# A hybrid decoder layer: the mixer's planned order, its state update and its DMA places are changed

## The chip, the cores and the metric

The kernel runs on one core of a Trainium2 chip. The metric is the time of one execution on the device, in microseconds (us). Lower is better.

## The reference

One layer on x of 1024 tokens by 1024 columns, all in float32, in this order:

```python
x = layer_norm(ALPHA * x + 0.5 * swiglu(x, ffn1_w_gu, ffn1_w_down))       # FFN 1, inner width 2816
z = x @ w_in                                                              # 3872 columns
# retention, 8 heads of 64, chunks of 128 tokens
scores = einsum('bnihd,bnjhd->bnhij', q, k) * intra                       # decay mask
state  = chunk_decay * state + einsum('bnjhd,bnjhe,hj->nbhde', k, v, k_decay)
ret    = scores @ v + (q * q_decay) @ previous_state                      # group norm, gate
# RWKV-7, 8 heads of 64, token by token
sa     = einsum('bhvk,bhk->bhv', state, kk)
state  = state * w - sa (x) (kk * a) + v (x) k
y      = einsum('bhvk,bhk->bhv', state, r)                                # group norm, bonus, gate
x = layer_norm(ALPHA * x + concat(ret, rw) @ w_out)
x = layer_norm(ALPHA * x + 0.5 * swiglu(x, ffn2_w_gu, ffn2_w_down))       # FFN 2
x = x + sigmoid(x @ ple_w_gate + b) * (p @ ple_w_proj)
```

kk is the key, scaled by rw_k_k and normalised to length 1 in each head: for that the squares of 64 columns are summed.

## The kernel before

Large products run as three float32r matmuls of high and low parts (mm3, lines 64 to 66); each operand is split by a ScalarE cast (line 50) and a VectorE or GpSimd subtraction (line 51). The two FFNs stand ahead of and behind the mixer, and the change doesn't touch them. The mixer lies at about 712 to 1584 us of the profiled span.

**Units.** Two heads and half of the sequence (512 tokens) make a unit, named w0_0 to w3_1 for RWKV and r0_0 to r3_1 for retention. A unit of RWKV is computed in four chunks of 128 tokens. For it the kernel needs, in this order:

- rw_inputs: the shifted mix of z, the decay, the squares of k (sq, line 1013), a matmul over them (line 1017), the normalised kk.
- rw_operands: the matmul m1p (line 1055) whose masked result M1 (line 1057) is a strictly lower triangle for each chunk and head; transposes of v, b and k (line 1069).
- substitution: inverts the 32 diagonal blocks of 32x32 of I - M1. M1 goes to a scratch in DRAM (line 1080) and comes back block by block (ilt, line 1084); 31 steps of two VectorE instructions follow (lines 1093 and 1095); the result ix goes to a second scratch (scs, line 1098).
- doublings: brings the blocks back into Xd (line 1108), transposes them on VectorE (line 1110) and joins them into the inverse of 128x128 by five groups of small matmuls, i1 to i5 (lines 1118 to 1140).
- rw_chunks, for each chunk: scores (lines 1152 and 1155), rhs (lines 1185 and 1188, copied by ScalarE on line 1190), sa = inverse times rhs (line 1194, copied on line 1196), the new state (lines 1200 and 1201), the output Y (lines 1213 to 1218). The state is kept in three tiles wst. The new one is fe * (PSUM + old state): ScalarE scales the old state (sf, line 1209), VectorE scales the PSUM result and adds (line 1210). The PSUM tile ch of a chunk holds rhs, sa, the state and Y side by side in one bank.
- rw_tail: group norm, transposes (ytp), the gate; the result goes to DRAM (mixed, line 1238).

**Fillers.** The projection z (28 column blocks of 48 matmuls, z_fill) and, after it, the product with w_out (wopo, 384 matmuls, w_out_fill) are cut into small pieces. w_out_fill loads its operands (line 1254) from mixed and w_out, splits them into mw, and adds each tile to xacc, which w_out loads from x1 (8 DMAs of 512 KB, line 1334).

**What sets the order.** The mixer's parts are generators. A `yield n` says that the part wants to go on n us later, on a planned clock that counts TensorE's work alone. The loop in `mixer` takes the part with the lowest rank that is due: 0 is the recurrence (doublings, chunks, tail), 1 the inputs and operands of the next unit, 2 the retention, -1 the substitution. Work done adds SHARE times its planned length to a debt, and while there is debt, or nothing is due, a piece of filler is taken. URGENT gives the instructions of a rank a higher or a lower priority for the scheduler that orders VectorE, ScalarE, GpSimd and the DMA queue. TensorE's instructions stay in the planned order. SP issues nearly all DMAs, in order: one that waits for its buffer holds back those behind it.

Of the kernel before, what the change touches and what calls it, by code (L numbers as in the profile page):

```python
# [28 lines left out]
SHARE = 0.65  # L29
URGENT = {-1: -60, 0: 60}  # L30


class Layer:
# [761 lines left out]
    def lora(self, zd, h):  # L795

        nc = self.nc
        sl = slice(h * HALF, (h + 1) * HALF)
        sg = []
        for i, (mu, omu) in enumerate(((self.pc("mu", 12), self.pc("omu", 12)), (self.pc("mu", 13), self.pc("omu", 13)),  # L800
                                       (self.pc("mu2"), self.pc("omu2")))):
            z = self.load_z(f"zl{i}_{h}", zd[i], h)
            t = self.ring("t", f"lt{i}_{h}")
            d = self.ring("t", f"ld{i}_{h}")
            self.shift_mix(d, z, mu, omu, t)
            if i == 0:
                nc.scalar.activation(d[0:64], d[0:64], AF.Tanh)
                nc.sync.dma_start(self.lor[:, sl], d)
            else:
                nc.scalar.activation(t, d, AF.Tanh, scale=0.5)  # L810
                nc.vector.tensor_scalar(out=d, in0=t, scalar1=0.5, scalar2=0.5, op0=ALU.mult, op1=ALU.add)
                sg.append(d)
        yield 8
        up = [self.mb.tile([P, HALF], F32, tag=t, name=f"gup{t}{h}", bufs=1) for t in ("zq", "zk")]
        nc.sync.dma_start(up[0], self.A["rw_g_up"][0][0:P])
        nc.gpsimd.memset(up[1][0:96], 0.0)
        nc.sync.dma_start(up[1][96:128], self.A["rw_g_up"][0][P:])
        for u in range(4):
            us = slice(u * P, (u + 1) * P)
            ps = self.ptile("sc", f"gps{u}_{h}", 2)  # L820
            for i in range(2):
                nc.tensor.matmul(ps, up[i][:, us], sg[i], start=i == 0, stop=i == 1)
            g = self.ring("c", f"gs{u}_{h}")
            nc.scalar.copy(g, ps)
            nc.sync.dma_start(self.gates[u][:, sl], g)
            yield 1
# [29 lines left out]
    def retention(self, u, h, zd, out):  # L856
# [83 lines left out]
        yield 9  # L940
# [14 lines left out]
    def rw_inputs(self, W, n, u, h, zd):  # L955
# [21 lines left out]
        k, r, v = m  # L977

# [33 lines left out]
        sq = tmp("sq")  # L1012
        nc.scalar.activation(sq, k, AF.Square, scale=self.pc("rw_k_k", u))
# [60 lines left out]
    def substitution(self, w):  # L1074
# [10 lines left out]
        yield 6  # L1085
# [3 lines left out]
        for j in range(B - 1):  # L1089
# [6 lines left out]
            yield 0.95  # L1096
        w.scr2 = self.dpool.tile([4, 8, B, B], F32, tag="scr2", name=f"scs{nm}", bufs=2)
        nc.sync.dma_start(w.scr2.rearrange("b s i j -> (b s) i j"), x)
        w.inverse = True
        self.substituting = False  # L1100

    def doublings(self, w):
# [3 lines left out]
        for b in range(4):  # L1106
            bs = slice(B * b, B * b + B)
            nc.sync.dma_start(self.Xd[bs, :, bs], w.scr2[b].rearrange("s i j -> i s j"))
# [6 lines left out]
        yield 8  # L1115
# [48 lines left out]
    def rw_chunks(self, w, out):  # L1164
# [6 lines left out]
        yr = self.ring("c", f"yr{nm}")  # L1171
        yield 3
        for c in range(4):
# [4 lines left out]
            if h == 1 and c == 0:  # L1178
                for e in range(2):
                    rr = slice(64 * e, 64 * e + 64)  # L1180
                    nc.vector.tensor_scalar(out=st[rr, rr], in0=st[rr, rr], scalar1=w.fm[rr, 0:1], scalar2=None, op0=ALU.mult)
# [17 lines left out]
            if not (h == 1 and c == 3):  # L1199
                nc.tensor.matmul(ch[:, 2 * P:3 * P], kt[:, cs], vt[:, cs], start=True, stop=False)  # L1200
                nc.tensor.matmul(ch[:, 2 * P:3 * P], bt[:, cs], sa, start=False, stop=True)
                for e in range(2):
                    rr = slice(64 * e, 64 * e + 64)
                    ps = ch[rr, 2 * P + 64 * e:2 * P + 64 * e + 64]
                    if first:
                        nc.vector.tensor_scalar(out=nx[rr, rr], in0=ps, scalar1=fe[rr, c:c + 1], scalar2=None, op0=ALU.mult)
                    else:
                        sf = mb.tile([P, 64], F32, tag="sf", name=f"sf{nm}{c}{e}", bufs=2)
                        nc.scalar.activation(sf[rr], st[rr, rr], AF.Copy, scale=fe[rr, c:c + 1])
                        nc.vector.scalar_tensor_tensor(out=nx[rr, rr], in0=ps, scalar=fe[rr, c:c + 1], in1=sf[rr],  # L1210
                                                       op0=ALU.mult, op1=ALU.add)
# [9 lines left out]
            yield 2.4  # L1221
# [3 lines left out]
    def rw_tail(self, w, yr, out):  # L1225
# [3 lines left out]
        yield 9  # L1229
# [8 lines left out]
        nc.sync.dma_start(out[:, sl], t)  # L1238
# [10 lines left out]
    def w_out_operand(self, kind, i, half, src):  # L1249
# [3 lines left out]
        raw = self.w_out_raw(f"wo{self.uid()}")  # L1253
        self.nc.sync.dma_start(raw, src)
# [3 lines left out]
    def w_out_fill(self, blocks, mixed, finish):  # L1258
# [4 lines left out]
        def operands(b):  # L1263
# [3 lines left out]
            if (ks, h) not in m:  # L1267
                m[ks, h] = [self.w_out_operand(0, i, h, mixed[k][:, h * HALF:(h + 1) * HALF]) for i, k in enumerate(ks)]
# [6 lines left out]
        yield 6  # L1275
# [9 lines left out]
        finish()  # L1285
# [3 lines left out]
        yield 5  # L1289
# [16 lines left out]
    def mixer(self, x1T, zs, mixed, x1, normalise):  # L1306
# [4 lines left out]
        with self.pool("zp") as zp, self.pool("mc") as mc, self.pool("mb") as mb, self.pool("mp", space=PSUM) as mp:  # L1311
# [7 lines left out]
            self.zdone, self.mixed_done = set(), set()  # L1319
            self.tail_done, self.hold, self.substituting = True, False, False  # L1320
# [8 lines left out]
            def w_out():  # L1329
# [3 lines left out]
                for t in range(TT):  # L1333
                    nc.sync.dma_start(self.xacc[t], x1[t * P:(t + 1) * P, :])
                yield from self.w_out_fill([(ks, h, n) for ks in ((4, 0), (5, 1), (6, 2), (7, 3)) for h in range(2)
# [67 lines left out]
            for s in range(-1, 9):  # L1403
# [14 lines left out]
                while any(t[1] in main for t in threads):  # L1418
# [3 lines left out]
                    if fg and (fready <= clock and (not able or debt > 0)):  # L1422
# [298 lines left out]
```

## Time and profile before

| | us |
|---|---|
| median of 3 runs | 2368.34 |
| lowest, highest | 2363.91, 2370.89 |
| profiled execution | 2372.27 |
| its span (first to last instruction) | 2370.20 |
| mean granted TensorE clock, share of full speed | 0.964 |

The profile names instructions by line, engine, operation and tile. A float32 matmul is recorded as two instructions, a float32r matmul or a transpose as one. A matmul's own duration overlaps the next one's: what it takes from TensorE is read from one start to the next. "Idle before" is time in which an engine stood still, put down to the releaser that came last. [...]

### The profile page before, as it was taken

How to read it: one execution, taken by the hardware profiler on the slowest of the kernel's cores; microseconds unless marked ns; L12 is line 12 of the kernel's file. 1: busy time of each engine (PE TensorE's matmuls, PEld its weight loads, DVE VectorE, ACT ScalarE, POOL GpSimd, SP SyncE). 2: the span in 40 equal slices, each digit the busy share in tenths (PEclk: the TensorE clock that was granted, in tenths of full speed). 3: DMA queues.
4: the chain of work that ended last, by engine and by line, in shares of the span. 5: the costliest groups of instructions: out<-in, count | busy, mean ns of one | idle time of the engine just before them, and what ended most of it. 6: DMA issues, size and time to landing. Idle time of an engine off the chain costs nothing.

```text
span 2370.2 us, 31197 instructions
## 1 busy us (share of the span) xinstructions
PE 2206.1 (93%) x11009; PEld 1793.0 (76%) x11009; DVE 1654.7 (70%) x2825; ACT 867.7 (37%) x1514; POOL 491.7 (21%) x384
## 2 busy tenths in 40 slices
PE   7999999999998989898998869778999999999999
PEld 5888888788785767776776757656888888788777
DVE  7777777665782477667757669769777767866862
ACT  4332323244643424324324323244323232445550
POOL 3345454100111000000000000016554553000220
PEclk9999999999999999999898879889999999999999
DMA  4355555597245433343243352032455554975321
GB/s 143 121 169 189 168 173 165 182 323 231 68 162 168 143 104 109 100 119 117 76 122 119 93 161 89 26 131 83 153 191 161 190 164 134 351 256 155 111 76 41
DMA packets 288963, 345.97 MB, mean 146 GB/s; under 512 B 35715, under 2 KB 162150, under 8 KB 288806
## 3 DMA queue, kind: packets, MB, share of 16 engines
q1 hardware_dynamic: 284224, 331.34, 43.7%
q0 software_dynamic: 3328, 12.06, 1.3%
q8 instruction: 87, 1.43, 0.3%
q10 hardware_dynamic: 1254, 0.58, 0.1%
q14 instruction: 70, 0.57, 0.1%
HBM read 237.47 MB, written 106.43 MB: 145 GB/s over the span
## 4 chain that ended last, share of the span: by engine, by line
PE 45%; DVE 11%; DMA 4%; ACT 3%; issue 2%; SPq 0%; POOL 0%; DVEq 0%; POOLq 0%; ACTq 0%
PE f2m L64 4%; PE f2m L65 3%; PE f2m L66 3%; PE z L64 3%; PE z L65 3%; PE z L66 3%; DMA f2w<-in_ffn_w_gu 2%; PE f2qa L65 1%; PE f2qa L66 1%; PE f2qa L64 1%; PE pg L65 1%; PE pg L64 1%; PE pg L66 1%; PE wopo L64 1%; PE wopo L65 1%
## 5 line engine op out<-in xcount | busy, mean ns | idle before, releaser
L64 PE MATMUL z<-x1Th,win_0h 128*128 128x512 f32 x224 | 103.2, 461 | 0.0
L64 PE MATMUL z<-x1Th,win_1h 128*128 128x512 f32 x224 | 100.2, 447 | 0.0
L66 PE MATMUL z<-x1Th,win_0l 128*128 128x512 f32 x224 | 91.5, 409 | 0.9 <-DVE win_0l L51 0.9
L65 PE MATMUL z<-x1Tl,win_0h 128*128 128x512 f32 x224 | 91.3, 407 | 0.0
L65 PE MATMUL z<-x1Tl,win_1h 128*128 128x512 f32 x224 | 91.1, 407 | 0.0
L66 PE MATMUL z<-x1Th,win_1l 128*128 128x512 f32 x224 | 91.1, 407 | 0.0
L152 POOL TENSOR_TENSOR f2tb<-f2tb,f2tb 128x512 f32<-128x512 f32 x44 | 70.5, 1601 | 91.6 <-DMA f2tb<-in_ffn_w_down 86.6
L51 DVE TENSOR_TENSOR f1hl<-f1s,f1hh 128x512 fp32r<-128x512 f32 x63 | 45.6, 723 | 61.7 <-ACT f1hh L50 61.7
L1095 DVE TENSOR_TENSOR ixw<-ixw,itw 32x31 f32<-32x31 f32 (+15 forms) x248 | 81.5, 329 | 6.2
L1093 DVE TENSOR_TENSOR itw<-iltw,ixw 32x31 f32<-32x31 f32 (+15 forms) x248 | 81.0, 327 | 6.3 <-issue 0.7
L64 PE MATMUL wopo<-mw 128*128 128x512 f32 x128 | 55.9, 437 | 23.9 <-ACT mw L50 23.7
L51 DVE TENSOR_TENSOR f2hl<-f2s,f2hh 128x512 fp32r<-128x512 f32 x63 | 45.0, 715 | 45.8 <-ACT f2hh L50 45.8
L1087 POOL MEMSET ixw<- 32x1024 f32 x8 | 7.5, 943 | 325.5 <-DMA scsw<-ixw 325.5
L50 ACT CAST f1hh<-f1s 128x512 fp32r<-128x512 f32 x63 | 39.2, 622 | 91.8 <-PE f1qa L65 38.3
L50 ACT CAST f2hh<-f2s 128x512 fp32r<-128x512 f32 x63 | 39.2, 623 | 90.4 <-PE f2qa L65 35.9
L152 POOL TENSOR_TENSOR f1tb<-f1tb,f1tb 128x512 f32<-128x512 f32 x44 | 64.8, 1474 | 32.6 <-DMA f1tb<-in_ffn_w_down 24.6
L111 DVE TENSOR_TENSOR f2S<-f2w 128x512 f32<-128x512 f32 x22 | 20.8, 947 | 65.1 <-DMA f2w<-in_ffn_w_gu 65.1
L65 PE MATMUL f2qa<-f2vl,f2hh 128*128 128x512 f32 x164 | 64.0, 390 | 0.5 <-DVE f2vl L51 0.5
L66 PE MATMUL f2qa<-f2vh,f2hl 128*128 128x512 f32 x164 | 63.9, 390 | 0.0
L65 PE MATMUL f1qa<-f1vl,f1hh 128*128 128x512 f32 x164 | 63.9, 389 | 0.0
L66 PE MATMUL f1qa<-f1vh,f1hl 128*128 128x512 f32 x164 | 63.8, 389 | 0.0
L182 DVE TENSOR_TENSOR f1U<-f1m,f1U 128x512 f32<-128x512 f32 x50 | 33.5, 687 | 42.7 <-PE f1m L66 42.6
(792 smaller groups left out, 7215.8 us busy)
## 6 DMA issues: line engine op xcount, KB each, us to landing
f1w<-in_ffn_w_gu SPq DMA_DIRECT2D x44, 512.0 KB
f2w<-in_ffn_w_gu SPq DMA_DIRECT2D x44, 512.0 KB
f1s<-hd SPq DMA_DIRECT2D x63, 256.0 KB
f2s<-hd SPq DMA_DIRECT2D x63, 256.0 KB
zs<-zs SPq DMA_DIRECT2D x56, 256.0 KB
raw_win<-in_w_in SPq DMA_DIRECT2D x54, 256.0 KB
f1tb<-in_ffn_w_down SPq DMA_DIRECT2D x44, 256.0 KB
wt<-f1tb SPq DMA_DIRECT2D x44, 256.0 KB
```

The source lines that it names most:

```text
L50: self.last_split = self.nc.scalar.copy(hi, src).ins
L51: (eng or self.nc.vector).tensor_tensor(out=lo, in0=src, in1=hi, op=ALU.subtract)
L64: mm(ps, a[0], b[0], start=first, stop=False)
L65: mm(ps, a[0], b[1], start=False, stop=False)
L66: mm(ps, a[1], b[0], start=False, stop=last)
L111: sub = lambda o, a, b, op=ALU.subtract: V.tensor_tensor(out=o, in0=a, in1=b, op=op)
L152: nc.gpsimd.tensor_tensor(out=t, in0=a, in1=b, op=ALU.subtract)
L182: add = lambda out, a, b, eng=V: eng.tensor_tensor(out=out, in0=a, in1=b, op=ALU.add)
L1087: nc.gpsimd.memset(x, 0.0)
L1093: nc.vector.tensor_tensor(out=t, in0=lt[:, j, j + 1:].unsqueeze(2).broadcast_to([B, n, c]), in1=x[:, j:j + 1, 0:c].broadcast_to([B, n, c]) ...
L1095: nc.vector.tensor_tensor(out=x[:, j + 1:, 0:c], in0=x[:, j + 1:, 0:c], in1=t, op=ALU.add)
```

## The change

- The planner: SHARE falls from 0.65 to 0.4; the substitution loses its lowered priority (-60); a filler piece is no longer taken for debt while a part of rank 0 is due; and nine of the `yield` values differ or go.
- sq is made in rw_inputs right behind the shifted mix, ahead of the `yield 4`.
- The loads into Xd are issued at the end of substitution, right behind the write of the second scratch, with `yield 12` behind them. They were at the head of doublings, with `yield 8`.
- The old state is added in PSUM, by a matmul with the identity (line 1203 of the changed kernel), and ScalarE writes the new state from PSUM with the scale fe (line 1207): two instructions of 64x64. sf and the two VectorE instructions go.
- The scaling of the state by fm at the start of a half is issued before the `yield 3`.
- The x1 loads into xacc are issued on GpSimd's queue, behind the first four operand loads of w_out.
- The last unit's output stays in SBUF (self.kept) and is split from there. The layer norm of the first half (finish) is issued behind the last operands.

```diff
-SHARE = 0.65
-URGENT = {-1: -60, 0: 60}
+SHARE = 0.4
+URGENT = {0: 60}
...
-        yield 8
+        yield 8 if h else 18
...
         k, r, v = m
+        sq = tmp("sq")
+        nc.scalar.activation(sq, k, AF.Square, scale=self.pc("rw_k_k", u))
 
         yield 4
...
-        yield 6
+        yield 8
         x = mb.tile([B, B, B], F32, tag="ix", name=f"ix{nm}", bufs=1)
...
-            yield 0.95
+            yield 0.4
         w.scr2 = self.dpool.tile([4, 8, B, B], F32, tag="scr2", name=f"scs{nm}", bufs=2)
         nc.sync.dma_start(w.scr2.rearrange("b s i j -> (b s) i j"), x)
...
+            nc.sync.dma_start(self.Xd[bs, :, bs], w.scr2[b].rearrange("s i j -> i s j"))
+        yield 12
+        w.inverse = True
...
-        yield 8
         ps = self.ptile("sc", f"i1{nm}", 2)
...
+                if not first:
+                    nc.tensor.matmul(ch[:, 2 * P:3 * P], self.ident, st, start=False, stop=False)
                 nc.tensor.matmul(ch[:, 2 * P:3 * P], bt[:, cs], sa, start=False, stop=True)
                 for e in range(2):
                     rr = slice(64 * e, 64 * e + 64)
-                    ps = ch[rr, 2 * P + 64 * e:2 * P + 64 * e + 64]
-                    if first:
-                        nc.vector.tensor_scalar(out=nx[rr, rr], in0=ps, scalar1=fe[rr, c:c + 1], scalar2=None, op0=ALU.mult)
-                    else:
-                        sf = mb.tile([P, 64], F32, tag="sf", name=f"sf{nm}{c}{e}", bufs=2)
-                        nc.scalar.activation(sf[rr], st[rr, rr], AF.Copy, scale=fe[rr, c:c + 1])
-                        nc.vector.scalar_tensor_tensor(out=nx[rr, rr], in0=ps, scalar=fe[rr, c:c + 1], in1=sf[rr],
-                                                       op0=ALU.mult, op1=ALU.add)
+                    nc.scalar.activation(nx[rr, rr], ch[rr, 2 * P + 64 * e:2 * P + 64 * e + 64], AF.Copy, scale=fe[rr, c:c + 1])
...
-        nc.sync.dma_start(out[:, sl], t)
+        if (u, h) == (3, 1):
+            self.kept = t
+        else:
+            nc.sync.dma_start(out[:, sl], t)
...
-        yield 6
+        residual()
+        yield 9
...
-        finish()
         while not ready(last):
             yield 1
         operands(last)
-        yield 5
+        finish()
+        yield 4
...
+                        nc.gpsimd.dma_start(self.xacc[t], x1[t * P:(t + 1) * P, :])
...
-                    if fg and (fready <= clock and (not able or debt > 0)):
+                    if fg and fready <= clock and (not able or debt > 0 and all(t[0] for t in able)):
```

Three places show what the change moves. On TensorE, in the second chunk of unit w0_0, before (kt and vt are token-major operands, bt the b vectors, arw the decayed keys and queries, scz the masked scores):

```order
L1200 MATMUL chw0_01_7747<-wvtw0_0_6785,wktw0_0_6826 128x128
L1201 MATMUL chw0_01_7747<-saw0_01_7777,wbtw0_0_6804 128x128
L1213 MATMUL chw0_01_7747<-wst1_6159,arw0_0_6717 128x128
L1217 MATMUL chw0_01_7747<-wvtw0_0_6785,scz2_6151 128x64
L1218 MATMUL chw0_01_7747<-saw0_01_7777,scz2_6151 128x64
```

And now:

```order
L1201 MATMUL chw0_01_7654<-wvtw0_0_6812,wktw0_0_6852 128x128
L1203 MATMUL chw0_01_7654<-wst1_6159,ident_58 128x128
L1204 MATMUL chw0_01_7654<-saw0_01_7691,wbtw0_0_6836 128x128
L1209 MATMUL chw0_01_7654<-wst1_6159,arw0_0_6746 128x128
L1213 MATMUL chw0_01_7654<-wvtw0_0_6812,scz2_6151 128x64
L1214 MATMUL chw0_01_7654<-saw0_01_7691,scz2_6151 128x64
```

One matmul with the identity (line 1203) is new; there are 24 of them, one for each chunk that has an old state and makes a new one. Line 1209 waited for VectorE (as line 1213 of before) and now waits for ScalarE.

On ScalarE, in the third chunk of unit w0_1, before (sa is the copy that line 1201 needs, yr the output's):

```order
L1196 COPY saw0_12_8652<-chw0_12_8626 128x128
L792 ACTIVATE smkw2_0_9124<-wzkw2_0_9120,pder_1851 128x512
L1219 COPY yrw0_1_8330<-chw0_12_8626 128x128
L50 CAST win2304_1h_8707<-raw_win2304_1_8618 128x512
L690 COPY zs2816_1_8701<-z2816_1_8506 128x512
```

And now:

```order
L1197 COPY saw0_12_8506<-chw0_12_8469 128x128
L842 ACTIVATE gsqr0_1_8455<-gnyr0_1_8451 128x512
L50 CAST win1664_1h_8534<-raw_win1664_1_8396 128x512
L690 COPY zs1152_1_8531<-z1152_1_8170 128x512
L844 ACTIVATE gstr0_1_8450<-gstr0_1_8450,col2_7327 128x8
L938 ACT_TABLE_LOAD
L938 ACTIVATE rthr0_1_8463<-zgr0_1_8461 128x512
L1207 ACTIVATE wst1_6159<-chw0_12_8469,few0_1_6960 64x64 x2
L1215 COPY yrw0_1_8139<-chw0_12_8469 128x128
```

The state copies (line 1207) stand behind the retention's group norm and a table load.

On SP's queue, around the second scratch of unit w2_1, before (scs is the scratch, ix the inverted blocks):

```order
L966 DMA lor0w3_1_11410<-lor_6167 128x512
L882 DMA zvr2_1_11200<-zs_65 128x512
L1234 DMA gtw2_0_11266<-gates_6168 128x512
L664 DMA raw_win1920_0_11252<-in_w_in 128x4x128
L1036 DMA bv_6169<-rkw3_0_11100 128x512
L691 DMA zs_65<-zs896_0_11208 128x512
L787 DMA wzvw3_1_11427<-zs_65 128x513
L1098 DMA scsw2_1_11102<-ixw2_1_10518 32x1024
L691 DMA zs_65<-zs896_1_11223 128x512
L664 DMA raw_win1920_1_11474<-in_w_in 128x4x128
L1108 DMA Xd_6143<-scsw2_1_11102 32x8x32 x4
```

And now:

```order
L787 DMA wzrw3_1_11399<-zs_65 128x513
L968 DMA lorww3_1_11390<-in_rw_w_up 64x128
L969 DMA lorww3_1_11390<-in_rw_a_up 64x128
L1098 DMA scsw2_1_10771<-ixw2_1_10495 32x1024
L1228 DMA bvw2_0_11074<-bv_6169 128x512
L1101 DMA Xd_6143<-scsw2_1_10771 32x8x32 x2
L1230 DMA gtw2_0_11076<-gates_6168 128x512
L1101 DMA Xd_6143<-scsw2_1_10771 32x8x32 x2
L871 DMA zqr2_1_11185<-zs_65 128x512
```

The write of the scratch no longer stands behind the loads of the unit's tail (gtw) and the next unit's (lor0w, zvr), and the Xd loads follow it with two DMAs of others between.

## Rows read from the trace of the kernel before

**Rows 1.** The windows view of the mixer; columns: stretch, length, busy us, clock, DMA, GB/s.

```profile
712.00:1584.00 872.00, 754.55 (x4564) 602.55 (x4563) 578.63 (x1348) 297.72 (x589) 20.47 (x61) 0.92 0.37 113
```

**Rows 2.** The waits of TensorE in the mixer: us in total, times, longest.

```profile
PE wopo L64 <- ACT mw L50: 23.7, 2, 16.9
PE i1w L1118 <- DMA Xd<-scsw: 23.1, 8, 9.9
PE chw L1213 <- DVE wst L1210: 20.0, 24, 1.2
PE sspw L1017 <- ACT sqw L1013: 19.2, 8, 4.2
PE gps L822 <- DMA raw_win<-in_w_in: 7.7, 1, 7.7
PE ytpw L853 <- DVE gnyw L846: 4.8, 1, 4.8
```

**Rows 3.** The windows view of stretches right behind five of these waits.

```profile
733.70:742.00 8.30, 8.21 (x16) 4.14 (x17) 2.69 (x4) 3.35 (x7) 0.00 (x0) 0.66 0.49 170
1386.70:1397.00 10.30, 10.02 (x32) 7.69 (x33) 7.00 (x12) 1.46 (x3) 1.09 (x2) 0.61 0.33 88
1556.80:1571.00 14.20, 7.38 (x23) 5.72 (x24) 5.57 (x8) 1.24 (x2) 0.00 (x0) 0.58 0.71 204
1342.00:1352.00 10.00, 9.95 (x41) 8.72 (x42) 6.88 (x19) 2.77 (x5) 0.00 (x0) 0.58 0.20 62
993.00:1000.00 7.00, 6.78 (x30) 6.19 (x32) 5.07 (x15) 2.74 (x6) 0.00 (x0) 0.59 0.14 45
```

**Rows 4.** TensorE's timeline in one chunk: start, us, line, tiles, idle before.

```profile
1352.72 0.39 PE L66 MATMUL z<-x1Th,win_0l 128*128 128x512 f32 x1
1352.95 0.38 PE L1200 MATMUL chw<-wvtw,wktw 128*128 128x128 f32 x2
1353.17 0.39 PE L1201 MATMUL chw<-saw,wbtw 128*128 128x128 f32 x2
1354.32 0.49 PE L1213 MATMUL chw<-wst,arw 128*128 128x128 f32 x2 [0.76 <-DVE wst L1210]
```

**Rows 5.** The state's tile wst, two of its groups: ns min/median/max, first and last start.

```profile
L1209 ACT ACTIVATE sfw<-wst,few x48: 335/344/348, 907.2 to 1539.1; 64x64 f32<-64x64 f32 x48
L1210 DVE SCALAR_TENSOR_TENSOR wst<-chw,few,sfw x48: 261/284/292, 918.0 to 1545.5; 64x64 f32<-64x64 f32 x48
```

**Rows 6.** ScalarE's groups in the mixer, one table load of several groups: busy, mean ns.

```profile
L1019 ACT ACT_TABLE_LOAD x8 | 10.3, 1283 | 0.1
```

**Rows 7.** The page's groups of the substitution's two instructions: busy, mean ns.

```profile
L1095 DVE TENSOR_TENSOR ixw<-ixw,itw 32x31 f32<-32x31 f32 (+15 forms) x248 | 81.5, 329 | 6.2
L1093 DVE TENSOR_TENSOR itw<-iltw,ixw 32x31 f32<-32x31 f32 (+15 forms) x248 | 81.0, 327 | 6.3 <-issue 0.7
```

**Rows 8.** VectorE's timeline, unit w0_0: first and last step, the transpose of Xd.

```profile
833.30 0.17 DVE L1093 TENSOR_TENSOR itw<-iltw,ixw 32x31 f32<-32x31 f32 x1
...
873.07 0.18 DVE L1095 TENSOR_TENSOR ixw<-ixw,itw 32x31 f32<-32x31 f32 x1
878.94 1.25 DVE L1110 STREAM_TRANSPOSE XTw<-Xd 128x1024 f32<-128x1024 f32 x1 [5.68 <-DMA Xd<-scsw]
```

**Rows 9.** VectorE's timeline, unit w2_1: the last step of its substitution.

```profile
1275.39 0.18 DVE L1095 TENSOR_TENSOR ixw<-ixw,itw 32x31 f32<-32x31 f32 x1
```

**Rows 10.** SP's timeline, unit w2_1: the second scratch and the loads into Xd.

```profile
1291.65 0.58 SPq L1098 DMA_DIRECT2D scsw<-ixw  x1
...
1296.19 1.81 SPq L1108 DMA_DIRECT2D Xd<-scsw  x4
```

**Rows 11.** The chain that ended last, at the mixer's end: start, us, what.

```profile
1559.51 1.99 DMA mixed<-wow
...
1561.51 2.50 DMA wo<-mixed
```

**Rows 12.** The windows view around the start of w_out.

```profile
1366.00:1400.00 34.00, 16.40 (x68) 13.16 (x69) 15.72 (x28) 7.43 (x15) 1.09 (x2) 0.65 0.65 200
```

More of the change, by code (lines that the diff above doesn't have):

```diff
@@ L939, in retention @@
         nc.vector.scalar_tensor_tensor(out=th, in0=th, scalar=1.0, in1=zg, op0=ALU.add, op1=ALU.mult)
-        yield 9
+        yield 12
         yt = self.transposes(y, f"ytp{nm}")
@@ L1010, in rw_inputs @@
         nc.vector.tensor_scalar(out=ath, in0=ath, scalar1=0.5, scalar2=0.5, op0=ALU.mult, op1=ALU.add)
-        sq = tmp("sq")
-        nc.scalar.activation(sq, k, AF.Square, scale=self.pc("rw_k_k", u))
         yield 5
@@ L1095, in substitution @@
             nc.vector.tensor_tensor(out=x[:, j + 1:, 0:c], in0=x[:, j + 1:, 0:c], in1=t, op=ALU.add)
-            yield 0.95
+            yield 0.4
         w.scr2 = self.dpool.tile([4, 8, B, B], F32, tag="scr2", name=f"scs{nm}", bufs=2)
         nc.sync.dma_start(w.scr2.rearrange("b s i j -> (b s) i j"), x)
+        for b in range(4):
+            bs = slice(B * b, B * b + B)
+            nc.sync.dma_start(self.Xd[bs, :, bs], w.scr2[b].rearrange("s i j -> i s j"))
+        yield 12
         w.inverse = True
@@ L1105, in doublings @@
         B = 32
-        for b in range(4):
-            bs = slice(B * b, B * b + B)
-            nc.sync.dma_start(self.Xd[bs, :, bs], w.scr2[b].rearrange("s i j -> i s j"))
         XT = mb.tile([P, 8, P], F32, tag="XT", name=f"XT{nm}", bufs=1)
@@ L1171, in rw_chunks @@
         yr = self.ring("c", f"yr{nm}")
+        if h == 1:
+            st = self.wst[4 % 3]
+            for e in range(2):
+                rr = slice(64 * e, 64 * e + 64)
+                nc.vector.tensor_scalar(out=st[rr, rr], in0=st[rr, rr], scalar1=w.fm[rr, 0:1], scalar2=None, op0=ALU.mult)
         yield 3
@@ L1177, in rw_chunks @@
             nx = self.wst[(4 * h + c + 1) % 3]
[L1178 to L1181, printed above, removed]
             ch = self.ptile("ch", f"ch{nm}{c}", 2)
@@ L1220, in rw_chunks @@
             E = F
-            yield 2.4
+            yield 2.2
         self.tail_done = False
@@ L1228, in rw_tail @@
         y = self.group_norm(yr, 64e-5, nm, "c")
-        yield 9
+        yield 13
         yt = self.transposes(y, f"ytp{nm}", "sc")
@@ L1252, in w_out_operand, with w_out_fill @@
         parts = [self.mw[:, 4 * kind + 2 * i + e, fs] for e in range(2)]
-        raw = self.w_out_raw(f"wo{self.uid()}")
-        self.nc.sync.dma_start(raw, src)
+        raw = self.kept
+        if src is not None:
+            raw = self.w_out_raw(f"wo{self.uid()}")
+            self.nc.sync.dma_start(raw, src)
         self.split(*parts, raw)
         return parts
-    def w_out_fill(self, blocks, mixed, finish):
+    def w_out_fill(self, residual, blocks, mixed, finish):
         nc = self.nc
@@ L1267, in operands @@
             if (ks, h) not in m:
-                m[ks, h] = [self.w_out_operand(0, i, h, mixed[k][:, h * HALF:(h + 1) * HALF]) for i, k in enumerate(ks)]
+                m[ks, h] = [self.w_out_operand(0, i, h, mixed[k][:, h * HALF:(h + 1) * HALF] if (k, h) != (7, 1) else None)
+                            for i, k in enumerate(ks)]
             if (ks, n) not in w:
@@ L1319, in mixer @@
             self.zdone, self.mixed_done = set(), set()
+            self.kept = None
             self.tail_done, self.hold, self.substituting = True, False, False
@@ L1332, in w_out, with residual @@
                 self.wo_tags = [("wraw", 2)] * 2 + [(f"wA{i}{e}", 1) for i in range(2) for e in "hl"] + [("zst", 2)] * 2
-                for t in range(TT):
-                    nc.sync.dma_start(self.xacc[t], x1[t * P:(t + 1) * P, :])
-                yield from self.w_out_fill([(ks, h, n) for ks in ((4, 0), (5, 1), (6, 2), (7, 3)) for h in range(2)
+                def residual():
+                    for t in range(TT):
+                        nc.gpsimd.dma_start(self.xacc[t], x1[t * P:(t + 1) * P, :])
+                yield from self.w_out_fill(residual, [(ks, h, n) for ks in ((4, 0), (5, 1), (6, 2), (7, 3)) for h in range(2)
                                             for n in range(2)], mixed, lambda: normalise(mb))
```

## The prediction

> **What bounds the kernel now.** I read the page for the shares of the engines, then the windows view of the mixer, then the waits of TensorE there, then timelines at the longest waits. The mixer is the part whose order changes. In it TensorE is busy for 754.6 of 872 us at a granted clock of 0.92 [rows 1]; VectorE for 578.6, ScalarE for 297.7. So TensorE bounds it, with two losses: 117 us (872 less 754.6) in which it stands still, and a clock that is at the lower level (0.5) for about 16% of the time. Both are to be had, since z and w_out are work that needs no waiting, if it stands in the right places.
>
> The standing still has few causes [rows 2]. Six lines hold 98.5 of the 117 us: the first operands of w_out (23.7 in two waits), the inverted blocks (23.1), the state (20.0), the squares (19.2), the LoRA matmuls of the gate (7.7), the last group norm (4.8). After a stall the clock is low [rows 3]: behind the wait at 733.7 us it is 0.66, behind the long one at 1386.7 it is 0.61, behind two of the squares' waits 0.58 and 0.59. What a low clock costs is TensorE's busy time there times (1 - clock): 8.21 x 0.34 = 2.8 us, 10.02 x 0.39 = 3.9, 7.38 x 0.42 = 3.1, 9.95 x 0.42 = 4.2, 6.78 x 0.41 = 2.8, which is 16.8 us behind these five.
>
> **The change, part by part.**
>
> *Squares first.* Today the square is queued on ScalarE behind the exponentials and all eight units wait for it, 19.2 us [rows 2]. Now it is issued two yields earlier, and line 1017 needs nothing else. Of the 19.2 I leave 1.2. What is late next is the square root behind it, a table load of 1.28 us [rows 6] and some small steps; the transposes that need them still stand 6 planned us later. Between -10 and -19 us; I take -18.
>
> *The gate's LoRA matmuls.* The yield of 18 instead of 8 puts 10 us more of z ahead of them; the wait was 7.7 us [rows 2]. I take -7.7; the other end is 0, if the load is as late again on SP's queue.
>
> *Start of w_out and the mixer's end.* The two waits for mw are 16.9 us and, as the rest of 23.7, 6.8 us [rows 2]. In the first, 4 MB of x1 are ahead of the operands on SP's queue, and the window moves 200 GB/s [rows 12], so 4.19 MB take 21 us. Now the operands go first, and by the order 48 small matmuls of the next unit, some 4 us, stand between the last of z and the first of w_out, where nothing stood. What is left is like the other wait of this group, 6.8, less some of that cover: 5 us. In the last wait, 1.99 us of writing and 2.50 of reading go since the tile is kept [rows 11]: 6.8 - 4.5 = 2.3. Ahead of it the wait of 4.8 for the last group norm gets 36 matmuls of w_out as cover by the order; at 0.23 us from start to start [rows 4] that is 8.3 us, more than the 4.8. Together 28.5 becomes 7.3: -21.2, between -12 and -26. The layer norm of the first half is now issued later; it lies beside the last 48 matmuls of w_out (11 us), and if it outlasts them FFN 2 starts some 2 us late, which the range holds.
>
> [...] No row here shows x1 on GpSimd's queue. [...]
>
> *Inverse blocks.* The 31 steps take 31 x (0.327 + 0.329) = 20.3 us by themselves [rows 7], but in unit w0_0 they last from 833.3 to 873.25, 40 us [rows 8], so as much again is other units' VectorE work between them; 5.7 us later VectorE gets the blocks. In unit w2_1 the last step ends at 1275.6, yet the scratch is written at 1291.65 and Xd loaded from 1296.19 [rows 9, 10]: 16 us of waiting in SP's queue. The change shortens this chain. By the order, the VectorE instructions of others between M1 and the last step fall from 522 to 372 over the eight units; at roughly 0.6 us each (20 us of others' work by 31 of them in w0_0) that is 90 us, 11 a unit. SP's detour in w2_1 goes too. But the cover falls as well: between the last m1p matmul and the first i1 stand 1140 filler matmuls in all, where 1449 stood, and fewer of the other matmuls: 309 x 0.23 = 71 us of filler, and with the rest some 100, 13 a unit. It is uneven: w1_1 has 249 now (162 before), and w1_0, w2_0, w3_0 have 96, 96 and 93 (162, 162, 144). So the chain and its cover shrink alike. In w0_0, w0_1 and w1_0 the transpose of Xd now follows the last step on VectorE with nothing between, as before only in w0_0, where VectorE stood 5.68 us for it [rows 8], and in w3_1. I expect 27 us of waits in place of 23.1: +4. The ends: -20 if the detours on SP were the cause, +37 if all six units with less cover wait 10 us, as w3_1 does today (longest 9.9 [rows 2]).
>
> *State in PSUM.* The 24 identity matmuls cost 0.22 us each, as line 1200 does from its start to the next one's [rows 4]: +5.3. VectorE's two instructions of 0.284 become ScalarE's two; the nearest row is sf, 0.344 from SBUF [rows 5]. Line 1213 waits for them because the write of Y and the state share a bank's tile: 24 waits, 0.83 on average. So 24 x 2 x 0.06 = +2.9. Behind a waiting copy stands whatever ScalarE has in its queue: in the order, six chunks have a table load and up to four 512-column operations between sa and the state copy. TensorE has about 3 us of its own between those two. I add 1 us for each of the six, +6 (0 to 2.5 each). Together +14, between +2 and +20. VectorE gains 48 x 0.284 = 14 us, which is off the path but is in the counts above.
>
> [...] No row here has a scaled ScalarE copy from PSUM of 64 columns; I stay with the row.
>
> *Clock.* The stalls behind which rows 3 show 16.8 us of loss mostly go, and no others as long come. I take -17; 0 to -30.
>
> **The sum**: -18 - 7.7 - 21.2 + 4 + 14.2 - 17 = -45.7. The profiled execution is 2372.3 us, so 2326.6. It is 3.9 us above the median of the three runs; against the median the forecast is 2323 us.
>
> **The rivals.**
>
> *The blocks are late everywhere.* SHARE and the shorter yields take filler from ahead of i1. For it: the cover of three units falls by a third or more, and the planner counts 0.4 us for a step that takes 0.66. Against it: the chain gets shorter too, and VectorE is busy for only two thirds. Six waits of 10 us are +37 over today in place of +4, and a low clock behind five more of them, 2.8 each at the cheapest of rows 3, less what they overlap, +10: 2323 + 33 + 10 = 2366.
>
> *ScalarE becomes the recurrence's bound: slower.* It executes in order, and now stands twice more in each chunk's path. If each of the 28 pairs is held by 2.5 us (a table load of 1.28 and two operations of 0.6), the waits are 70 us more: 2323 + 70 - 6 already counted = 2387. It decides from 1.6 us a pair on (45 / 28). Against it: ScalarE is busy for 34% of the mixer [rows 1], and 18 of the 24 chunks have no table load there.
>
> *x1 holds up w_out from the other queue.* The 16.9 us stay [rows 2], with their clock: +12 and +4: 2339. For it: the window is at a DMA share of 0.65 already [rows 12]. Against: the operands are issued first.
>
> *The whole chain comes early.* i1 waits only 3 us (-24), the state's waits stay at 20 (-9), and the clock gives 8 more: 2282. For it: the detour on SP's queue cost 16 us in one unit.
>
> **How the numbers follow.** Forecast 0.56, late blocks 0.14, ScalarE 0.10, x1 0.06, whole chain 0.14. A difference below 0.3% (7 us) can't be told from none. Faster by more than that: 0.54 + 0.03 + 0.06 + 0.14 = 0.77; the same: 0.02 + 0.09 = 0.11; slower: 0.02 + 0.10 = 0.12. The forecast's own range, its bounds taken as independent, is 2298 to 2350. The range of eight in ten goes from 2288, short of the best case, to 2368, just beyond the late blocks.
>
> **What would show it.** In the waits of TensorE of the changed kernel: line 1017 behind sq under 3 us in all; gps gone; the first wopo wait 3 to 8 us and the last under 4; i1 20 to 35 us; line 1209 behind ScalarE 25 to 35 us. The clock over the mixer 0.94 or more, and the mixer some 45 us shorter. I am wrong if i1 waits over 50 us, if line 1209's waits exceed 50, or if new waits on VectorE or on xacc take the place of those that went.

## The result: slower, 2386 us, and the profile after

The changed kernel takes 2386.2 us (median of 4 runs, 2383.3 to 2389.5), the kernel before 2367.3 in the same runs: a ratio of 1.008, 95% interval 1.0058 to 1.0102. The forecast was 2323 us, with a range of 2288 to 2368: wrong in sign.

All of it lies in the mixer. The first matmul of FFN 2's transposes starts at 1593.4 us, where it started at 1577.6 (+15.8); from there to the end both take 793 us. The windows view shows the mixer, and two stretches right behind waits for the inverted blocks (columns as in [rows 1]):

```profile
712.00:1600.00 888.00, 749.27 (x4616) 606.10 (x4614) 560.44 (x1288) 297.09 (x596) 24.37 (x68) 0.92 0.36 110
866.40:875.60 9.20, 7.53 (x56) 6.24 (x55) 5.77 (x10) 3.39 (x4) 0.00 (x0) 0.50 0.18 57
1410.30:1420.00 9.70, 8.85 (x97) 8.12 (x98) 5.70 (x8) 0.00 (x0) 0.00 (x0) 0.50 0.64 197
```

TensorE is busy for as long as before [rows 1] and stands longer; the clock hasn't risen: 0.50 behind these two waits, lower than behind any of [rows 3]. The waits of TensorE in the mixer:

```profile
PE i1w L1118 <- DMA Xd<-scsw: 70.0, 11, 15.3
PE chw L1209 <- ACT wst L1207: 24.9, 24, 2.3
PE vtpr L853 <- DMA zvr<-zs: 13.0, 2, 6.9
PE wopo L64 <- DVE xacc L1305: 6.7, 4, 4.2
PE ytpr L853 <- DVE gnyr L846: 4.9, 3, 2.6
PE wopo L64 <- ACT mw L50: 3.0, 1, 3.0
PE chw L1213 <- ACT wst L1207: 3.0, 4, 0.8
```

Against [rows 2]: the waits for the squares (19.2), the gate (7.7) and the last group norm (4.8) are gone, those for mw fell from 23.7 to 3.0 (6.7 on xacc are new). Two causes took more than that: the inverted blocks, 23.1 to 70.0, and 13.0 for zvr, a load of the retention.

Unit w0_0 shows how. TensorE's timeline, its last filler and the first two pieces of i1, then VectorE's: M1, first and last step and the transpose of Xd (start, us):

```profile
851.13 0.40 PE L66 MATMUL z<-x1Th,win_1l 128*128 128x512 f32 x1
866.01 0.44 PE L1118 MATMUL i1w<-Xd,M 64*64 64x64 f32 x2 [14.48 <-DMA Xd<-scsw]
867.04 1.23 PE L1118 MATMUL i1w<-Xd,M 64*64 64x64 f32 x18 [0.58 <-DMA Xd<-scsw]
```
```profile
804.93 1.35 DVE L1057 COPY_PREDICATED M<-mask,m1pw 128x512 f32<-128x512 uint8 x2 [0.97 <-PE m1pw L1055]
...
826.38 0.17 DVE L1093 TENSOR_TENSOR itw<-iltw,ixw 32x31 f32<-32x31 f32 x1
...
861.53 0.18 DVE L1095 TENSOR_TENSOR ixw<-ixw,itw 32x31 f32<-32x31 f32 x1
867.08 1.25 DVE L1111 STREAM_TRANSPOSE XTw<-Xd 128x1024 f32<-128x1024 f32 x1 [5.36 <-DMA Xd<-scsw]
```

In the kernel before, M1 and the first piece of i1 in the same unit:

```profile
810.13 1.33 DVE L1057 COPY_PREDICATED M<-mask,m1pw 128x512 f32<-128x512 uint8 x2
...
878.16 0.44 PE L1118 MATMUL i1w<-Xd,M 64*64 64x64 f32 x2 [7.25 <-DMA Xd<-scsw]
```

The steps last 35.3 us, 4.6 less than in [rows 8], but TensorE is at i1 already at 851.5 (866.01 less 14.48). M1 was ready at 806.3, so the cover, the time until TensorE gets to i1, is 45.2 us; before it was 59.5. The table has this for all units, read from the timelines of VectorE, SP and TensorE, in us. The chain goes from the end of M1 to the end of SP's issue of the last load into Xd (the blocks are there some 1.5 us later: in w0_0 the issue ends at 865.5, and i1 goes on at 867.0). The cover goes from the end of M1 to the end of TensorE's last instruction ahead of i1. A unit is late where its cover is shorter than its chain.

| kernel | chain, mean of 8 units | cover, mean of 8 units | late units, and by how much in all | i1 waits in all |
|---|---|---|---|---|
| before | 82.6 | 87.4 | 4, by 18.3 | 23.1 |
| before, step 0.4 | 73.2 | 84.1 | 2, by 30.9 | 33.0 |
| after | 69.2 | 68.4 | 6, by 58.9 | 70.0 |
| after, step 0.95 | 75.2 | 83.8 | 1, by 3.7 | 6.0 |
| after, yield 29 behind Xd | 69.6 | 88.5 | 2, by 9.2 | 14.3 |
| after, low priority | 71.4 | 64.8 | 6, by 99.9 | 106.2 |
| after, SHARE and filler rule as before | 60.7 | 80.3 | 2, by 18.0 | 22.4 |

The waits follow the late units and not the means: the lateness, and for each late unit 1 to 2.5 us until the blocks have landed, make the last column. Cover that one unit has to spare, as w1_1 has 36 us after the change, helps no other. The rows "before" and "after" are the two kernels of the change; the others are experiments below.

In w3_0 the Xd loads themselves were late. SP's queue, from the scratch to the last load:

```profile
1386.92 0.34 SPq L1098 DMA_DIRECT2D scsw<-ixw  x1
...
1389.87 0.95 SPq L1101 DMA_DIRECT2D Xd<-scsw  x2
...
1403.12 0.43 SPq L1101 DMA_DIRECT2D Xd<-scsw  x1
...
1407.23 0.43 SPq L1101 DMA_DIRECT2D Xd<-scsw  x1
```

Twelve us of other DMAs, most of them w_out's operands, stand between the halves, and 3.7 us more ahead of the last load. In the kernel before, SP held this unit too: the last step ended at 1367.7, and the scratch was issued 20 us later,

```profile
1387.80 0.38 SPq L1098 DMA_DIRECT2D scsw<-ixw  x1
```

but its cover was 109 us, and i1 did not wait; now it is 66. So the detour of [rows 10] is gone in w2_1, but not that of w3_0.

The state's tile wst in after (ns min/median/max, first and last start), against [rows 5]:

```profile
L1207 ACT ACTIVATE wst<-chw,few x56: 293/309/311, 899.4 to 1555.9; 64x64 f32<-64x64 f32 x56
```

### The profile page after: what moved, and what is told of

The parts are those of the page before. It is cut to its first block, busy times and chain, and to the rows that moved or that the text cites. A ratio compares the mean times of both kernels' runs of the same rounds, so it can differ in the third digit from the quotient of the medians.

```text
span 2386.2 us, 31214 instructions
## 1 busy us (share of the span) xinstructions
PE 2199.6 (92%) x11057; PEld 1795.1 (75%) x11057; DVE 1633.2 (68%) x2769; ACT 866.6 (36%) x1522; POOL 497.0 (21%) x392
## 5 line engine op out<-in xcount | busy, mean ns | idle before, releaser
L1118 PE MATMUL i1w<-Xd,M 64*64 64x64 f32 x256 | 16.4, 290 | 70.0 <-DMA Xd<-scsw 70.0
L1118 PEld LDWEIGHTS i1w<-Xd,M 64*64 64x64 f32 x256 | 14.2, 197 | 74.2 <-DMA Xd<-scsw 59.1
L111 DVE TENSOR_TENSOR f2S<-f2w 128x512 f32<-128x512 f32 x22 | 22.4, 1016 | 68.7 <-DMA f2w<-in_ffn_w_gu 64.1
```

The lines of the kernel that those rows point to most:

```text
L111: sub = lambda o, a, b, op=ALU.subtract: V.tensor_tensor(out=o, in0=a, in1=b, op=op)
L1118: nc.tensor.matmul(ps[r, 64 * i:64 * i + 64], w.M1[r, i, r], self.Xd[r, i, r], start=True, stop=True)
```

## The experiments

P names the theory that the planned step of 0.4 lets TensorE reach i1 before the blocks are there.

**The planned step: 0.95, 0.7, 1.2.** One number of the changed kernel, in substitution:

```diff
-            yield 0.4
+            yield 0.95
```

> The changed kernel with one number put back: the planner counts 0.95 us for a step of the substitution, not 0.4. Theory P (the planner promises the inverse too early, so i1 stands too early in TensorE's order): the 70 us of waits at i1 fall below 30, and the time falls by 30 to 50 us, to 2335 to 2355, below the kernel before. Rival S (the state copies on ScalarE are what costs): the waits at line 1209 stay at 25 us, i1's waits may move, and the time stays within 10 us of 2386. Rival D (the substitution's restored priority on VectorE delays all others): i1's waits fall, but waits on VectorE grow by as much, and the time stays above 2370.

Measured: 2308.4 us, ratio to before 0.9755 [0.9719, 0.9792]. The waits, and the window up to the mixer's end:

```profile
PE chw L1209 <- ACT wst L1207: 17.8, 24, 0.9
PE ytpw L853 <- DVE gnyw L846: 6.5, 1, 6.5
PE i1w L1118 <- DMA Xd<-scsw: 6.0, 2, 5.8
```
```profile
712.00:1515.00 803.00, 733.48 (x4595) 589.61 (x4593) 543.30 (x1272) 299.13 (x591) 23.49 (x66) 0.96 0.39 121
```

One number is worth 78 us. i1's waits go from 70.0 to 6.0, the clock from 0.92 to 0.96, and this kernel beats both: in the mixer TensorE stands 67 us less and, at the higher clock, is busy for 11 us less. With 0.7 and 1.2 in place of 0.95:

> The changed kernel with 0.7 us a step, between 0.4 (70 us of waits at i1, 2386) and 0.95 (6 us, 2308). Theory P: in between, i1's waits 15 to 45 us and the time 2320 to 2355. Rival: a threshold or chance; the time is at one of the two ends, within 8 us of 2386 or 2308.

> The changed kernel with a step of 1.2 in place of 0.4. Theory P: i1's waits are nearly gone at 0.95 (6.0 us), so there is little left to gain: i1 0 to 6 us, 2300 to 2320 us, not to be told from 2308. Rival: cover is bought from the end of the mixer, and the recurrence, made later by 31 x 0.25 = 8 us a unit, runs past the filler there: 2325 us or more, with waits on the last units' chunks.

0.7: 2327.9 us, ratio 0.9833 [0.98, 0.9865]; i1 waits 11.9, and one wait of another kind is back:

```profile
1358.31 1.09 PE L853 MATMUL vtpr<-ident,zvr 128*128 128x128 f32 x4 [24.88 <-DMA zvr<-zs]
```

1.2: 2318.6 us, ratio 0.981 [0.9783, 0.9837], with 15.7 us of waiting at i1 in the last unit, where no filler was left, and 9.6 at one matmul of the retention (rspr, behind VectorE's kd); so i1's waits (20.5 in all) were above what P expected, and 0.95 stands near the best.

**The same cover from another place.** The step stays 0.4; the yield behind the Xd loads makes up for it:

```diff
-        yield 12
+        yield 29
         w.inverse = True
```

> The changed kernel with the step left at 0.4 and the yield behind the loads into Xd raised from 12 to 29. Planned time from the first step to the doublings is then 31 x 0.4 + 29 = 41.4 us, as with the step of 0.95 (31 x 0.95 + 12 = 41.5); only the pacing of the steps differs, which are issued as early as in the changed kernel. Theory P (the doublings come too early on TensorE, so that the cover is shorter than the chain): it does as well as the step of 0.95: i1 waits under 15 us, 2300 to 2325 us. Rival Q (what hurts is that the steps are issued in a bunch and sit badly in VectorE's queue): i1 waits over 35 us or as much appears behind other VectorE work, 2345 us or more.

Measured: 2351.4 us, ratio 0.9941 [0.9918, 0.9965]. i1 waits 14.3 us, as P says, but the time is 43 us above the step of 0.95. TensorE stands 37 us longer (107.3 against 70.1), and most of that is one wait:

```profile
PE vtpr L853 <- DVE ixw L1095: 27.1, 1, 27.1
PE i1w L1118 <- DMA Xd<-scsw: 14.3, 5, 5.5
```

The releaser named, a step of the next unit's inverse, makes no input of this transpose; SP's queue shows what does:

```profile
1345.63 0.41 SPq L875 DMA_DIRECT2D zqsr<-zs  x1
...
1372.96 0.82 SPq L875 DMA_DIRECT2D zqsr<-zs  x2
...
1378.40 0.42 SPq L882 DMA_DIRECT2D zvr<-zs  x1
```

Between two pieces of one rotated operand, 27.3 us apart (1345.63 and 1372.96), stand 10 loads of w_out and 9 scratch, ilt and Xd transfers; each that had to wait held back all behind it, and zvr came last, at 1378.40. To test it, the retention's input loads (lines 864 to 867, 871, 875, 882) go to GpSimd's queue:

```diff
-        nc.sync.dma_start(zv, v[:, sl])
+        nc.gpsimd.dma_start(zv, v[:, sl])
```

> The changed kernel with step 0.4, the yield of 29 behind the loads into Xd, and all of the retention's input loads (lines 864 to 867, 871, 875, 882) issued on GpSimd's queue. In the same kernel without that move (2351 us) one wait of TensorE for a retention transpose (vtpr) lasted 27.1 us: SP issued the first two of the rotated pieces at 1345 us, then the operands of w_out, the scratch and Xd loads of the inverse, each held for its own buffer, and zvr only at 1378.4 us. Theory H (SP's order holds the load): vtpr's waits fall from 30 to under 8 us and the time to 2305 to 2330 us. Rival (the load waits for z itself or for its buffer, whatever the queue): vtpr or ktpr still waits over 18 us, 2340 to 2360 us. Rival (GpSimd's queue is held by its own waits): other long waits come, 2360 us or more.

> The changed kernel with a step of 0.95 and the retention's input loads on GpSimd's queue: the attempt at the fastest version. With this step alone (2308 us) no retention wait over 2 us was seen, so theory H gives little: 2300 to 2312 us, i1 4 to 8 us, 10 us off SP's queue at most. Rival (GpSimd's queue, on which the x1 loads of xacc and the memsets of ix also stand, holds the loads): 2320 us or more.

With the yield of 29: 2338.2 us, ratio 0.9902 [0.9874, 0.9929]:

```profile
PE i1w L1118 <- DMA Xd<-scsw: 21.8, 5, 7.8
PE vtpr L853 <- DMA zvr<-zs: 9.5, 1, 9.5
```

vtpr's waits fell from 30.8 to 11.4 in all: SP's order held the load, but not for all of the wait. What is left shows in the same run, in the issue of the load on GpSimd's queue and in the windows view around it:

```profile
1355.18 0.54 POOL L882 DMA_DIRECT2D zvr<-zs  x1
```
```profile
1353.00:1365.00 12.00, 2.69 (x23) 1.91 (x21) 6.64 (x12) 3.48 (x7) 2.64 (x5) 0.75 0.97 321
```

zvr is issued 23 us sooner than on SP, right behind four of the x1 loads (2 MB), and TensorE gets it only at 1365.2, in a stretch in which the DMA engines are busy for 0.97. The time came down by 13 us (9 by the ratios), less than expected; the intervals overlap a little. With the step of 0.95 the same move gives 2315.7 us, ratio 0.9801 [0.9781, 0.9822], no gain over 2308: there was no such wait to remove.

**Priority of the substitution.**

```diff
-URGENT = {0: 60}
+URGENT = {-1: -60, 0: 60}
```

> The changed kernel with the lowered priority of the substitution (-60) restored, step 0.4. Theory P: the chain from M1 to Xd gets longer, the cover stays, so i1 waits more than 70 us: 2390 to 2420 us. Rival (the substitution at normal priority delays what TensorE needs from VectorE, and that is part of the loss): 2360 to 2380 us, with i1's waits no larger than 75.

Measured: 2397.8 us, ratio 1.0135 [1.0114, 1.0155]; `i1w` waits:

```profile
PE i1w L1118 <- DMA Xd<-scsw: 106.2, 12, 24.8
```

As P says, the chain is longer, by some 2 us a unit; the cover didn't stay but fell by some 4. At this step the normal priority is a gain.

**SHARE and the rule on rank 0, at either step.** The changed kernel with both as before:

```diff
-SHARE = 0.4
+SHARE = 0.65
...
-                    if fg and fready <= clock and (not able or debt > 0 and all(t[0] for t in able)):
+                    if fg and fready <= clock and (not able or debt > 0):
```

> The changed kernel with SHARE 0.65 and the old rule for fillers, the step left at 0.4. Theory P: more filler goes beside the recurrence, but the promise is still too early, so i1 still waits 40 us or more, and the time is 2355 to 2385. Rival W (SHARE is the cause): i1's waits fall below 20 us and the time below 2335.

> The changed kernel with a step of 0.95, SHARE 0.65 and the old rule for filler, so that of the planner's part only the priority of the substitution and the small yields stay changed. Theory P with the refinement that SHARE matters only where the cover is short: 2300 to 2325 us, i1 under 12. Rival (SHARE 0.4 and recurrence first are themselves a gain, since they save filler for later): 2330 us or more, with more waits behind ScalarE and VectorE in the chunks of the last units. Rival (they are a loss also at the right step): under 2298 us.

At step 0.4: 2355.4 us, ratio 0.9958 [0.9939, 0.9977], i1 waits 22.4, zvr 22.1. At step 0.95: 2321.1 us, ratio 0.9809 [0.9786, 0.9832], i1 waits 11.8. So the recurrence-first rule with SHARE 0.4 costs 31 us at the short step and gains some 12 at the long one (the intervals there overlap a little): it takes i1 up the moment that it is due, which is right only if the planned moment is.

**Parts put into the kernel before.** First the step of 0.4 alone:

```diff
-            yield 0.95
+            yield 0.4
```

> The converse: the kernel before with 0.4 us a step in the planner's count of the substitution in place of 0.95, and nothing else. Theory P (the promise alone sets how much cover i1 gets): the cover between M1 and i1 falls by about 15 us in most units, i1's waits rise from 23 to 50 to 90 us, and the time rises by 15 to 50 us, to 2380 to 2415. Rival W (the step count hurts only together with the new SHARE and the filler rule): i1's waits stay under 40 us and the time within 12 us of 2365.

Measured: 2386.0 us, ratio 1.008 [1.0051, 1.0108]:

```profile
PE i1w L1118 <- DMA Xd<-scsw: 33.0, 4, 22.1
PE vtpr L853 <- DMA zvr<-zs: 4.1, 1, 4.1
```

The time is as expected, the place only in part: i1's waits rise by 10 us, nearly all in w0_0 (22.1), since with the old SHARE and filler rule the other units still have 82 to 101 us of cover; w0_0 has 36.6. So the step alone takes the cover from one unit; together with the new SHARE and rule it takes it from most. TensorE stands 18 us longer; the rest, besides zvr, is spread thin and I can't name it. Then the Xd loads at the end of substitution with `yield 12`, as in the change, alone:

```diff
             yield 0.95
...
+        for b in range(4):
+            bs = slice(B * b, B * b + B)
+            nc.sync.dma_start(self.Xd[bs, :, bs], w.scr2[b].rearrange("s i j -> i s j"))
+        yield 12
         w.inverse = True
...
     def doublings(self, w):
...
-        for b in range(4):
-            bs = slice(B * b, B * b + B)
-            nc.sync.dma_start(self.Xd[bs, :, bs], w.scr2[b].rearrange("s i j -> i s j"))
...
-        yield 8
```

> The kernel before with the Xd loads at the end of the substitution and a yield of 12 behind them, in place of a yield of 8 at the head of the doublings. Theory P: cover and chain stay as long, the loads no longer stand behind others on SP's queue; i1's waits fall from 23 to 10 to 20 us, and the time by 0 to 15 us, to 2352 to 2367. Rival: moving the loads is itself what puts i1 too early; i1's waits grow above 40 us, and the time is above 2375.

Measured: 2377.9 us, ratio 1.0052 [1.0033, 1.0072]. A miss: the waits for i1 rose from 23.1 to 39.0 instead of falling. Issuing the loads earlier doesn't help where SP holds them: in w0_0 the scratch is written 5.3 us behind the last step, where it was 0.2, and in w3_0 36 us. The chain is 83.7 us a unit where it was 82.6, the cover 87.9 where it was 87.4. Then the squares, the gate's yield and the start and end of w_out together (the rest of its diff is what the change does with self.kept, w_out_operand, w_out_fill and the x1 loads):

```diff
-        yield 8
+        yield 8 if h else 18
...
         k, r, v = m
+        sq = tmp("sq")
+        nc.scalar.activation(sq, k, AF.Square, scale=self.pc("rw_k_k", u))
...
-        yield 6
+        residual()
+        yield 9
```

> The kernel before with three parts of the change: squares first, the gate's yield of 18, and the end of the mixer (x1 on GpSimd's queue, last output kept, layer norm later). Theory P: these are the parts that gain; the waits on sq, gps and mw (51 us before) fall to under 15, i1 stays near 23, and the time falls by 30 to 55 us, to 2312 to 2337. Rival (the removed waits come back at i1 or in VectorE, since the chain of the inverse sets the pace): the waits at i1 grow by 20 us or more, and the time stays within 15 us of 2367.

Measured: 2340.1 us, ratio 0.9892 [0.9848, 0.9935]. The waits for the squares and the gate are gone; those at i1 and for w_out are

```profile
PE i1w L1118 <- DMA Xd<-scsw: 34.9, 9, 11.0
PE ytpw L853 <- DVE gnyw L846: 6.5, 1, 6.5
PE wopo L65 <- DVE mw L51: 5.8, 1, 5.8
PE wopo L64 <- ACT mw L50: 2.9, 1, 2.9
PE wopo L64 <- DVE xacc L1309: 1.3, 2, 0.9
```

i1 waits 12 us more than before, though nothing of the inverse was touched: the chain is as long (82.7 us a unit), and the cover fell from 87.4 to 83.9, since waits that were removed had been cover. The other four rows are the start and end of w_out with the last group norm: 16.5 us, where 28.5 stood. And the state in PSUM alone, or taken out of the version with step 0.95:

```diff
+                if not first:
+                    nc.tensor.matmul(ch[:, 2 * P:3 * P], self.ident, st, start=False, stop=False)
...
-                        nc.scalar.activation(sf[rr], st[rr, rr], AF.Copy, scale=fe[rr, c:c + 1])
-                        nc.vector.scalar_tensor_tensor(out=nx[rr, rr], in0=ps, scalar=fe[rr, c:c + 1], in1=sf[rr],
-                                                       op0=ALU.mult, op1=ALU.add)
+                    nc.scalar.activation(nx[rr, rr], ch[rr, 2 * P + 64 * e:2 * P + 64 * e + 64], AF.Copy, scale=fe[rr, c:c + 1])
```

> The kernel before with the state in PSUM and its copies on ScalarE, and nothing else of the change. Theory P: 24 identity matmuls of 0.22 us are 5 us, and 24 waits of 1.04 in place of 0.83 us are 5 more: 0.2 to 0.6% slower, 2372 to 2382. Rival S: over 1% slower, above 2391, with the waits at line 1209 above 40 us.

> The changed kernel with 0.95 us a step and the old state update (sf on ScalarE, scale and add on VectorE), to price the state in the good schedule, 2308 with the state in PSUM. Theory P: without effect that can be told, 2300 to 2316, as it was in the kernel before (ratio 0.9997). Rival S: the state in PSUM costs or gains over 10 us here, below 2298 or above 2318.

Alone: 2364.8 us, ratio 0.9997 [0.9975, 1.0019]; no effect, where a loss of 5 to 14 us was expected. The waits for the state are 20.9 us in all (24.4 before), i1's 16.8, and TensorE is busy for 5.7 us more. Taken out at 0.95: 2311.9 us, ratio 0.9769 [0.974, 0.9799], not to be told from 2308.

**The square back at its old place**, in the changed kernel:

```diff
         k, r, v = m
-        sq = tmp("sq")
-        nc.scalar.activation(sq, k, AF.Square, scale=self.pc("rw_k_k", u))
...
+        sq = tmp("sq")
+        nc.scalar.activation(sq, k, AF.Square, scale=self.pc("rw_k_k", u))
         yield 5
         ps = self.ptile("ta", f"ssp{nm}", 2)
```

> The changed kernel with the square back at its old place behind the exponentials, all else as changed (step 0.4). Theory G (a wait of TensorE that stands between M1 and i1 is cover for the chain; to take it away shortens the cover by as much): line 1017 waits 15 to 20 us again, i1's waits fall from 70 to about 55 to 62, and the time is 2386 to 2400 us, so that early squares are worth 0 to 12 us here and not 18. Rival (the terms are independent): i1 stays at 70, the time is 2403 us or more.

Measured: 2379.7 us, ratio 1.0074 [1.0055, 1.0092]. Both expectations fall: line 1017 waits 2.5 us in all, not 15 to 20, and i1 68.0. The timeline, unit w1_0 (ScalarE's square, TensorE's use of it):

```profile
980.45 0.73 ACT L1013 ACTIVATE sqw<-wkw,pcol 128x512 f32<-128x512 f32 x1
991.85 1.00 PE L1017 MATMUL sspw<-ones,sqw 128*128 128x2 f32 x8
```

Here TensorE has 11 us of other work ahead of the sums, so the late square is hidden anyway. In the changed kernel the rest of the change is enough to take this wait away, and moving the square gains nothing measurable.

## Why the prediction was wrong, by its steps

- **Inverse blocks: the step that failed.** I put "So the chain and its cover shrink alike", by 11 and 13 us a unit, and the wait at +4. The chain shrank by 13.4 and the cover by 18.9 (table above), so that six units are late where four were, and the waits grew by 46.9. The chain's part was sized well; the cover was mis-sized. I counted it in matmuls of the order, 309 fillers and "some 100 us" in all; it was 151. The fillers came as counted (291 fewer between M1 and i1). But TensorE also stands still in that stretch: 79 us in all before and 54 after, so 25 us of the cover went with waits that other edits removed, and the count had no such term; the rest is TensorE's work other than filler. And I had seen that the planner counts 0.4 us for a step of 0.66 [rows 7], and used it only for a rival: 31 steps planned 17 us shorter a unit, which no VectorE instruction was. With 0.95 the cover is 15.4 us a unit longer. I also balanced means, where each unit has to be in time by itself. The sign that I had named for being wrong, i1 over 50 us, is the one that came.
- **The rival that came true** was "The blocks are late everywhere", at a chance of 0.14. It was priced at 2366 with 60 us of waits at i1. There were 70.0, and zvr's 13.0, a load that stands behind others in SP's order, were not in it.
- **Clock: wrong with it.** -17 was to come from stalls that go; as many came. It stayed at 0.92 over the mixer; without the waits at i1 it is 0.96.
- **Squares: right.** 19.2 fell to nothing. In the kernel before it is the edit that does it: with the three parts there line 1017 doesn't wait, with the Xd loads alone it waits 16.8 us. In the changed kernel the rest of the change does it too (2.5 us with the square late).
- **Gate: right.** 7.7 is gone (forecast -7.7).
- **w_out: near in number, in part by borrowing.** For w_out and its end 28.5 became 9.7 (forecast 7.3). But TensorE doesn't wait for the first operands, since it stands 15.1 us at i1 of w3_0 while they load. And the last group norm is hidden by 36 matmuls of w_out that are left at the end: 246 of 384 stand behind the last i1, where 138 stood before and 120 stand with the step of 0.95. They are the filler that is missing ahead of i1. Where i1 has its cover, that wait is back at 6.5 (step of 0.95). By the run of these parts in the kernel before, they are worth 28.5 less 16.5, -12, the low end of the stated range. The x1 rival did not come: in the mixer of the changed kernel no engine waits for an x1 load. The 6.7 on xacc are waits for VectorE, which adds late since it has the steps of w3_1 and the splits of mw to do without a pause; TensorE's longest one, and VectorE's last step and its add:

```profile
1473.27 0.80 PE L64 MATMUL wopo<-mw 128*128 128x512 f32 x1 [4.23 <-DVE xacc L1305]
```
```profile
1472.22 0.40 DVE L1095 TENSOR_TENSOR ixw<-ixw,itw 32x247 f32<-32x247 f32 x1
1472.55 0.67 DVE L1305 SCALAR_TENSOR_TENSOR xacc<-wopo,xacc 128x512 f32<-128x512 f32 x1
```

  What another queue gives, the retention's loads show: zvr, moved to GpSimd's queue, took 10 us to come (1355.18 to 1365.2) while the DMA engines were busy for 0.97. Whether x1's loads ahead of it on that queue or SP's beside them held it is not shown. What the move saved is not small: TensorE's waits for zvr fell by 19 us (30.8 to 11.4), because on SP it had stood in order behind other loads' waits.
- **State in PSUM: the sign of its waits wrong, and harmless.** Line 1209 behind ScalarE waits 24.9, where I had put 25 to 35; with line 1213 it is 27.9, for 24.4 behind VectorE before. But alone the edit makes these waits shorter (20.9) and changes nothing in the time, 0 ± 5 us for the +14 of the forecast; only its matmuls cost what I had put (5.7 us of TensorE's time for +5.3). The copy from PSUM took 309 ns (median, line 1207 after) against 344 for sf from SBUF [rows 5], the row that the forecast stayed with: it was 35 ns too long. ScalarE as the bound of the recurrence did not come: no wait there exceeds 2.3 us.

The measured parts of TensorE's standing: -19.2 - 7.7 - 18.8 + 46.9 + 13.0 for zvr, and about +7 in small waits (ytpr, line 1209 and others), make +21, from 115.4 to 136.6 us; 5 us less of busy time leave the +16 of the mixer. One sum of the forecast doesn't come out: the bounds of its terms, taken as independent (the root of the sum of the squares of their distances), give 2293 to 2363, not 2298 to 2350. 2386 lies outside of either.

## What to carry to other kernels

In a plan made ahead, the planned length of a side chain is cover for that chain: shortening it below what the instructions take moves the wait, it doesn't remove it. Judge each such number by slack, the time at which TensorE gets there less the time at which the result lands, unit by unit and not as a mean, and remember that a wait taken out elsewhere in that stretch takes cover out too, and that filler which is left over at the end is missing ahead of an earlier wait. And try a change's numbers one at a time: here a single one turned -2.4% into +0.8%.

## What the runs showed of the hardware

- SP's DMA queue, in order and shared by the loads of several parts, held one load back to 1378.40 while TensorE stood 27.1 us (yield of 29). Issued on GpSimd's queue 23 us sooner, at 1355.18, the same load left 9.5 us of waiting. The releaser that the trace names in the first case makes no input of that transpose; the queue's own timeline shows what held it.
- That load of 256 KB took 10 us from its issue to its use (1355.18 to 1365.2) in a stretch in which the DMA engines were busy for 0.97 and moved 321 GB/s.
- In windows of 1 us over the mixer the granted clock is 1.00 in 714 of 872 before and in 724 of 888 after, 0.50 in 124 and 132, and between the two in the rest. In the kernel before, behind the wait of 16.9 us for w_out's first operands, matmuls of 128x512 start 0.43 us apart at 0.50 (1392.91 to 1394.61) and 0.23 apart at 1.00 (1395.14 to 1396.96).
- In the changed kernel, behind waits of 14.5 and 15.1 us, the granted clock was 0.50 for the next 9 us, the lower of these two, though TensorE was busy for 7.53 and 8.85 us of them: as an estimate, half of that, 3.8 and 4.4 us, is what each stall cost on top.
- A scaled ScalarE copy of 64x64 from PSUM took 309 ns after (median of 56), 35 less than the one from SBUF before (344, median of 48).
